# A decoder layer on one core: the stretch from the state space's GLU to the second feed-forward in a held order

## The chip, the core and the metric

The kernel runs on one core of a Trainium2 chip. Its engines each run their own instruction queue: PE (TensorE, matrix products), DVE (VectorE), ACT (ScalarE), POOL (GpSimd) and SP (SyncE, which here only issues DMAs). The metric is the device time of one execution in microseconds, the median of several runs.

## The reference

One layer for one sequence of 1024 tokens and width 1024, all in float32: a feed-forward half-step, a mixing step, and a second feed-forward half-step. Each is normed before and after and modulated by columns computed from a vector `c`.

```python
h = modulate(rms_norm(x, g_pre_ff1[l]), sh1, sc1)
f = swiglu(h, w1_gate[l], w1_up[l], w1_down[l])
x = x + 0.5 * ga1[:, None, :] * rms_norm(f, g_post_ff1[l])

h = modulate(rms_norm(x, g_pre_mix[l]), sh2, sc2)
proj = h @ w_in[l]
...
ssm = s5_ssm(u, ...)          # ends: y = gelu(y); y = y * sigmoid(y @ w_glu + b_glu)
mixed = jnp.concatenate([rms_norm(attn, g_attn_out[l]), rms_norm(ssm, g_ssm_out[l])], axis=-1)
mixed = mixed @ w_out[l]
x = x + ga2[:, None, :] * rms_norm(mixed, g_post_mix[l])

h = modulate(rms_norm(x, g_pre_ff2[l]), sh3, sc3)
f = swiglu(h, w2_gate[l], w2_up[l], w2_down[l])   # (silu(h @ w_gate) * (h @ w_up)) @ w_down
x = x + 0.5 * ga3[:, None, :] * rms_norm(f, g_post_ff2[l])
```

## The kernel before

Every large product is made three times in a reduced form of float32: each operand is split into a high part, an ACT copy (`L69`), and a low part, a DVE subtraction (`L70`), and `mm3` issues high by high, high by low and low by high (`L74` to `L76`). One `mm3` over 512 columns is three matmuls.

On-chip memory is cut into named slots (`a0` to `a27`, `q0` to `q7`, `h0` to `h7`, `r0` to `r3`, `w0` to `w3`, `t0`, `t1`, `c0`), and PE's accumulator memory into banks `b0` to `b7`. A new tile in a slot waits until the old one's last reader is done. Most of the program's order is chosen by a scheduler that replays a timeline. Code inside `pinned(...)` keeps, on every engine, the order in which it is written. SP's queue is in order: a DMA that waits for its slot holds those behind it.

The stretch that is changed has these steps, for eight tiles of 128 tokens:

- *GLU.* Four weight blocks (`late.conv(4)` to `late.conv(7)`) times the split `y_hl`, in two halves of 512 tokens: eight results, each through a sigmoid (`L1214`), a product with `y_t` (`L1215`), a split into `mix_s` and a square summed into `sqs` (`L1221`, `L1222`). The second half of `w_out` comes through `shares`: load, ACT scaling (`L777`), DVE low part (`L778`).
- *Shares.* `share(t)` multiplies tile t of `mix_s` with `w_out`, two halves of four `mm3`; DVE adds it to the attention's share `acc[t]` (`L1254`), ACT squares it (`L1256`), DVE multiplies by the gate row (`L1257`).
- *Joined.* `joined(p)` norms a pair of tiles, adds the residual `X[t]` (`L1266`, slots `a10`, `a11`, `a13` in turn), stores it (`L1267`), squares it (`L1268`), norms again and scales `acc[t]` (`L1272`). `rsqrt` (`L144` to `L148`) is one ACT square root and four small DVE instructions.
- *Turn.* `turn(c, k)` transposes a block of 128 columns of tiles 4c to 4c + 3 on PE (`L1278`), and ACT writes it, modulated, into `hf[k]` (`L1279`).
- *First products.* The second feed-forward's gate and up products take seven Strassen products per pair of output blocks, but the first pair takes eight plain ones. `first(r, c)` is four `first_part`s of four `mm3` each; r is the token half and c the width half. `block(r, c, k)` splits their operands from `hf`. `first(0, ·)` needs only tokens 0 to 511.
- *The rest.* `rest` walks a list of steps (u, m), one product m of output block u each, 12 matmuls. The second pair, u = 2 and 3, comes as (2, "1"), (3, "1"), (2, "2"), (3, "2"), (2, "5") and so on. `wt.conv(i + 3)` converts weights ahead of step i. When a pair is complete `sums` makes four sums at once (`L535`). The operands `s1` to `s4` are sums of quarters of `hf`, made in `s12` and `s34`. A hook turns eight columns of `w_ada` into modulation columns (`L169`), on every second step from step 9.

Before, this stretch from the GLU to `first(1, 0)` is written without `pinned`, and the scheduler interleaves it.

## Time and profile before

| | |
|---|---|
| median of 3 runs | 1674.44 us (1672.31, 1674.44, 1674.67) |
| the profiled execution | 1673.76 us |
| its span | 1671.6 us, 21995 instructions |
| PE busy | 1641.9 us, 98% of the span |
| DVE, ACT, POOL busy | 1225.6, 818.2, 52.5 us |
| mean granted PE clock | 0.996 |
| moved by DMA | 248.53 MB, 149 GB/s on average |

The span runs from the first instruction to the last of the profiled execution; its own time has 2.2 us more. A row of the time order gives start, duration, engine, line, operation, result and operands, and in brackets the idle time before it with what ended it. A group's row gives the number of instructions, their busy time in us, the mean of one in ns, and the idle time before them. Line numbers are those of the kernel before.

### The profile page before, as it was taken

What the parts mean: (1) busy time and instruction counts of PE and PEld (TensorE: products, weight loads), DVE (VectorE), ACT (ScalarE), POOL (GpSimd) and SP (SyncE); (2) the same over time, 40 slices, a digit from 0 to 9 for tenths busy, and PEclk for the clock granted to TensorE, in tenths of its full rate; (3) what the DMA queues carried; (4) which work ended last, traced back from release to release, by engine and by line L of the source; (5) the groups of instructions that cost most, each with busy time, mean ns of one, the idle gap of its engine ahead of it and who ended that gap; (6) DMA issues with size and microseconds to landing.
All of it is one profiled execution on the core that took longest, in us unless ns stands there. A gap on an engine that the chain in (4) does not pass through costs nothing.

```text
span 1671.6 us, 21995 instructions
## 1 busy us (share of the span) xinstructions
PE 1641.9 (98%) x7715; PEld 1347.5 (81%) x7715; DVE 1225.6 (73%) x2277; ACT 818.2 (49%) x1601; POOL 52.5 (3%) x108
## 2 busy tenths in 40 slices
PE   8999999999999999999999998999999999999998
PEld 7878888787788888877887786878888888888886
DVE  6889998789969758758757475877656666578585
ACT  6643333463345458738753558533333333355462
POOL 0001110001100000000000000000000000000000
PEclk9999999999999999999999999999999999999999
DMA  9256762244396334520142225332322333593344
GB/s 368 81 208 230 254 227 99 95 146 152 123 331 243 115 118 145 210 101 26 51 145 65 97 102 199 121 144 95 107 95 95 118 116 114 163 364 104 107 141 136
DMA packets 110913, 248.53 MB, mean 149 GB/s; under 512 B 11962, under 2 KB 27618, under 8 KB 110803
## 3 DMA queue, kind: packets, MB, share of 16 engines
q1 hardware_dynamic: 101074, 213.60, 36.9%
q0 software_dynamic: 9152, 32.49, 5.8%
q8 instruction: 60, 0.98, 0.2%
q10 hardware_dynamic: 576, 1.05, 0.2%
q14 instruction: 51, 0.41, 0.1%
HBM read 187.35 MB, written 59.75 MB: 148 GB/s over the span
## 4 chain that ended last, share of the span: by engine, by line
PE 90%; DVE 5%; ACT 3%; issue 1%; DMA 1%; SPq 0%; DVEq 0%; ACTq 0%
PE b L74 27%; PE b L76 27%; PE b L75 27%; PE b L988 1%; PE b L886 1%; PE b L989 1%; PE b L990 1%; PE b L935 1%; DVE h L535 1%; PE b L1110 1%; DVE w L70 1%; PE b L1114 1%; PE b L1624 1%; ACT q L1533 1%; PE b L1068 0%
## 5 line engine op out<-in xcount | busy, mean ns | idle before, releaser
L74 PE MATMUL b<-a,w 128*128 128x512 f32 x1260 | 493.6, 393 | 6.0 <-ACT w L69 3.3
L76 PE MATMUL b<-a,w 128*128 128x512 f32 x1260 | 492.1, 391 | 1.8 <-DVE w L70 1.5
L75 PE MATMUL b<-a,w 128*128 128x512 f32 x1260 | 491.8, 390 | 1.3 <-DVE a L70 1.0
L74 PEld LDWEIGHTS b<-a,w 128*128 128x128 f32 x1260 | 237.4, 189 | 59.6 <-ACT w L69 4.9
L76 PEld LDWEIGHTS b<-a,w 128*128 128x128 f32 x1260 | 237.0, 188 | 53.9 <-DVE w L70 5.1
L75 PEld LDWEIGHTS b<-a,w 128*128 128x128 f32 x1260 | 237.0, 188 | 50.0 <-DVE a L70 1.5
L70 DVE TENSOR_TENSOR w<-r,w 128x512 fp32r<-128x512 f32 (+1 forms) x208 | 144.5, 696 | 132.1 <-ACT w L69 131.7
L75 PE MATMUL b<-w,r 128*128 128x512 f32 x528 | 205.5, 389 | 0.0
L76 PE MATMUL b<-w,r 128*128 128x512 f32 x528 | 205.4, 389 | 0.0
L74 PE MATMUL b<-w,r 128*128 128x512 f32 x528 | 182.0, 389 | 0.0
L69 ACT CAST w<-r 128x512 fp32r<-128x512 f32 (+1 forms) x208 | 129.0, 622 | 80.3 <-DVE r L403 67.7
L69 ACT CAST r<-a 128x512 fp32r<-128x512 f32 x110 | 68.4, 623 | 146.1 <-PE b L76 104.5
L70 DVE TENSOR_TENSOR r<-a,r 128x512 fp32r<-128x512 f32 x110 | 75.7, 689 | 75.9 <-ACT r L69 75.8
L75 PEld LDWEIGHTS b<-w,r 128*128 128x128 f32 x528 | 99.1, 188 | 20.7 <-DVE w L70 0.2
L74 PEld LDWEIGHTS b<-w,r 128*128 128x128 f32 x528 | 99.1, 188 | 20.6
L76 PEld LDWEIGHTS b<-w,r 128*128 128x128 f32 x528 | 99.1, 188 | 20.5
L69 ACT CAST w<-t 128x512 fp32r<-128x512 f32 (+1 forms) x114 | 69.9, 613 | 80.4 <-DVE t L406 29.9
L70 DVE TENSOR_TENSOR w<-t,w 128x512 fp32r<-128x512 f32 (+1 forms) x114 | 77.9, 683 | 31.1 <-ACT w L69 30.9
L560 ACT ACTIVATE h<-h 128x512 f32<-128x512 f32 x60 | 38.0, 633 | 121.7 <-DVE h L572 121.7
L572 DVE TENSOR_TENSOR h<-h,b 128x512 f32<-128x512 f32 x120 | 82.2, 685 | 20.6 <-PE b L76 18.6
L70 DVE TENSOR_TENSOR w<-a,w 128x512 fp32r<-128x512 f32 x110 | 75.3, 685 | 0.0
L74 PE MATMUL b<-a,a 128*128 128x512 f32 x182 | 72.2, 398 | 0.4 <-ACT h L1214 0.4
(419 smaller groups left out, 2437.5 us busy)
## 6 DMA issues: line engine op xcount, KB each, us to landing
r<-in_w_gu SPq DMA_DIRECT2D x87, 512.0 KB, 4.2
g_d<-h SPq DMA_DIRECT2D x154, 256.0 KB, 2.2
a<-g_d SPq DMA_DIRECT2D x110, 256.0 KB, 2.7
q<-in_w_ada POOLq DMA_DIRECT2D x48, 512.0 KB, 4.6
a<-in_w_d SPq DMA_DIRECT2D x88, 256.0 KB, 5.4
a<-in_w_ada SPq DMA_DIRECT2D x24, 512.0 KB, 9.1
a<-in_x SPq DMA_DIRECT2D x12, 512.0 KB, 5.3
x_d<-a SPq DMA_DIRECT2D x12, 512.0 KB, 3.2
```

What stands on the lines that cost most here:

```text
L69: act.copy(hi, src)
L70: eng.tensor_tensor(lo, src, hi.bitcast(F32), op=SUB)
L74: pe.matmul(psum, wh, xh, start=first, stop=False, skip_group_check=goes_on)
L75: pe.matmul(psum, wh, xl, start=False, stop=False, skip_group_check=goes_on)
L76: pe.matmul(psum, wl, xh, start=False, stop=last, skip_group_check=goes_on)
L535: dve.tensor_tensor(d, x, y, op=op)
L560: act.activation(dst, src, AF.Silu)
L572: dve.tensor_tensor(dst, dst, pb, op=ADD)
L886: pe.matmul(pb[kv][:, m % 2, ks], qT[m][rows, t * P : (t + 1) * P], kT[rows, (t + 1 - nk) * P : (t + 1) * P], start=True, stop=True,)
L935: pe.transpose(pt[:, m, :], pr[4 * kv + m][:, b * P : (b + 1) * P], ident)
L988: pe.matmul(pb, hh, wh, start=k == 0, stop=False)
L989: pe.matmul(pb, hh, wl, start=False, stop=False)
```

## The change

From the GLU on everything is inside `pinned`: `glu` and `both_shares` write out one order for all engines. In it

- all eight `X` tiles have slots of their own, and are loaded ahead;
- `rsqrt` can issue another piece of work between its root and its reciprocal, and `norm` takes the second norm of one pair and the first of another in one go;
- part of the scalings and of the blocks from `turn` moves from ACT to DVE;
- the first token half's transposes stand around share 7, and the second half's behind `first(0, 1)`, between the four first steps of the second pair, which stand ahead of `first(1, 0)`. Their weights have slots `a0` to `a3`;
- both token halves of the first pair use banks `b0` to `b3`;
- `s3` and `s4` are made in the rest's steps 4, 6 and 7, in exchanged slots;
- the pairs' sums are made one per step, those of the first pair from step 16 on;
- the modulation columns come from step 15 on, four in 14 steps, through two slots instead of six;
- `late.conv(4)`, `late.conv(5)` and `shares.load(4)` stand earlier in `middle`, and some slots are others.

```diff
-    def rsqrt(v, n):
+    def rsqrt(v, n, beside=None):
         act.activation(s, v, AF.Sqrt)
+        if beside:
+            beside()
         dve.reciprocal(y, s)
...
+        def rest(self, hook, pin, begin=0):
+            for i, (u, m) in enumerate(self.wt.seq):
+                if i >= begin:
+                    pin(self.wt.conv, i + 3)
+                    pin(self.step, u, m)
+                    if self.todo:
+                        pin(self.todo.pop(0))
+                    hook(i)
...
+            late.conv(4)
+            shares.load(4)
             ss_state(3)
...
-            late.conv(4)
-            shares.load(4)
             out_a(5)
+            late.conv(5)
...
+        def glu():
+            for j in range(8):
...
+                act.activation(y2, pb, AF.Sigmoid, bias=b_glu[:, m : m + 1])
                 dve.tensor_tensor(y2, y2, y_t[m][:, tk], op=MUL)
+                if j:
+                    glu_out(j - 1)
+                if j in (0, 1, 3, 5):
+                    shares.conv((0, 1, 3, 5).index(j))
+                if j in (2, 4):
+                    late.conv(5 + j // 2)
+                if j == 4:
+                    wt.load(0, 0)
+        X_TAGS = "q4", "q5", "q6", "q7", "a10", "a11", "a13", "a27"
...
+        def scaled(p, second=dve):
             for i in range(2):
+                t, r = 2 * p + i, R[p, 1][:, i : i + 1]
+                if i and second is dve:
+                    dve.tensor_scalar(acc[t], X[t], r, None, op0=MUL)
+                else:
+                    act.activation(acc[t], X[t], AF.Identity, scale=r)
+        def turned_in(c, k):
+            if k % 2 and (c == 0 or k < 4):
+                dve.tensor_scalar(dst, src, scale, shift, op0=MUL, op1=ADD)
+            else:
+                act.activation(dst, src, AF.Identity, scale=scale, bias=shift)
...
+        def both_shares():
...
+            share_all(4)
+            joined(3)
+            norm([(1, 0), (0, 1)], lambda: gated(3))
+            scaled(0, act)
+            share_all(5)
...
+            share_all(6)
+            norm([(1, 1)], lambda: gated(4))
+            scaled(1)
+            joined(5)
...
+            turn(0, 0)
+            turn(0, 1)
+            share(7, 0, range(4))
+            norm([(2, 0)], lambda: gated(5))
...
+            share(7, 1, range(4))
+            x_load(7)
...
+            for u, i in ((2, 0), (3, 0), (2, 1), (3, 1)):
+                wt.load(u, i)
+            g2.block(0, 1, 3)
+            added(2)
+            gated(7)
+            added(3)
+            for k in range(4):
+                g2.first_part(0, 1, k, (0, 1))
...
+            norm([(3, 1), (2, 1)], lambda: wt.conv(1))
+            scaled(2)
+            scaled(3)
+            wt.conv(2)
+            g2.step(2, "1")
+            turn(1, 0)
+            turn(1, 1)
...
+            g2.first_done(0)
+            wt.conv(3)
+            g2.step(3, "1")
...
+            g2.step(2, "2")
...
+            g2.step(3, "2")
...
+            g2.first(1, 0)
+            for k in range(4):
+                g2.block(1, 1, k)
+            g2.s1(0, 1, 2, 3)
+            g2.s2(0, 1, 2, 3)
+            wt.conv(8)
+            g2.first(1, 1)
+            g2.first_done(1, False)
...
     def hook3(i):
-        if i < 5:
+        if i == 4:
+            g2.s3(0, 1, 2, 3)
+        if i == 16:
+            z = slot("q2", [2, 512])
+            g2.todo.extend(g2.sums(0, [z[:, 1], g2.st[0, 1, 0], z[:, 0], g2.st[0, 0, 1]], True))
+        if i in (6, 7):
+            g2.s4(2 * i - 12, 2 * i - 11)
+        if i < 15:
             return
...
-        if last_raw and i > 8 and i % 2:
+        if last_raw and i % 14 in (5, 7, 9, 11):
             ada_block(*last_raw.pop(0), last_c[0])
...
-    g2.rest(lambda i: pinned(hook3, i), pinned)
+    g2.rest(lambda i: pinned(hook3, i), pinned, 4)
```

Three places of the resulting order. The first is SP's queue around the residual tiles, `x1_d` in memory; before:

```order
L379 DMA h0_1522_8965<-in_w2_gu 128x512
L379 DMA h1_1523_8966<-in_w2_gu 128x512
L1267 DMA x2_d_92<-a10_1467_8683 128x1024
L1267 DMA x2_d_92<-a11_1474_8720 128x1024
L1248 DMA a10_1492_8819<-x1_d_91 128x1024
L1267 DMA x2_d_92<-a13_1479_8755 128x1024
L1248 DMA a11_1497_8854<-x1_d_91 128x1024
L1267 DMA x2_d_92<-a10_1492_8819 128x1024
L1248 DMA a13_1510_8918<-x1_d_91 128x1024
```

and now (tiles 0 to 3, in `q4` to `q7`, are loaded ahead of these rows):

```order
L1268 DMA a10_1470_8697<-x1_d_91 128x1024
L1268 DMA a11_1471_8699<-x1_d_91 128x1024
L1268 DMA a13_1472_8701<-x1_d_91 128x1024
L1318 DMA x2_d_92<-q4_1453_8627 128x1024
L1318 DMA x2_d_92<-q5_1454_8629 128x1024
L1318 DMA x2_d_92<-q6_1455_8631 128x1024
L1318 DMA x2_d_92<-q7_1456_8633 128x1024
L1268 DMA a27_1539_9045<-x1_d_91 128x1024
L376 DMA r1_1562_9168<-in_w2_gu 128x1024
```

The loads no longer alternate with the stores whose slots they take, and the second pair's first raw weight stands behind tile 7. The second place is ACT's queue around the last pair's scaling (`a6` and `a8` are `acc[6]` and `acc[7]`); before:

```order
L1279 ACTIVATE q5_1458_8635<-b6_1557_9129,modc_77,gsc_78 128x512
L69 CAST a21_1561_9186<-q5_1458_8635 128x512
L1268 ACTIVATE a8_1405_8400,s1528_8998<-a11_1543_9071 128x1024
L144 ACTIVATE s1550_9098<-s1549_9096 128x2
L1279 ACTIVATE q6_1459_8636<-b7_1558_9147,modc_77,gsc_78 128x512
L1272 ACTIVATE a6_1397_8361<-a10_1526_8995,s1551_9099 128x1024
L1272 ACTIVATE a8_1405_8400<-a11_1543_9071,s1551_9099 128x1024
L69 CAST a22_1562_9189<-q6_1459_8636 128x512
L1279 ACTIVATE q7_1460_8637<-b6_1559_9153,modc_77,gsc_78 128x512
```

and now:

```order
L1319 ACTIVATE a6_1400_8367,s1531_9010<-a13_1472_8701 128x1024
L1319 ACTIVATE a8_1405_8400,s1531_9010<-a27_1539_9045 128x1024
L146 ACTIVATE s1568_9242<-s1567_9240 128x4
L71 CAST a0_1570_9245<-r1_1562_9168 128x512
L1327 ACTIVATE a4_1378_8240<-a10_1470_8697,s1569_9243 128x1024
L1327 ACTIVATE a6_1400_8367<-a13_1472_8701,s1569_9243 128x1024
L71 CAST a1_1571_9256<-r2_1563_9170 128x512
L589 COPY h2_1573_9272<-b4_1572_9259 128x512
L1343 ACTIVATE q0_1516_8963<-b6_1574_9274,modc_77,gsc_78 128x512
```

One root serves two pairs, the first token half's blocks (`q5` to `q7`) are gone from between, and the casts of the step weights `a0` and `a1` stand around the scalings. The third place is DVE's queue behind the second pair's last product; before:

```order
L564 TENSOR_TENSOR h0_1655_9795<-h0_1655_9795,b1_1623_9557 128x512
L535 TENSOR_TENSOR h7_1644_9693<-h2_1621_9551,h0_1655_9795 128x512
L535 TENSOR_TENSOR h3_1624_9570<-h0_1655_9795,h4_1633_9630 128x512
L535 TENSOR_TENSOR h5_1636_9649<-h3_1624_9570,h2_1621_9551 128x512
L535 TENSOR_TENSOR h1_1659_9817<-h6_1642_9676,h5_1636_9649 128x512
L169 ISA q0_1640_9658,modc_77<-q0_1640_9658,c0_1637_9651,cols_76 128x1024
L169 ISA modc_77 128x1
L70 TENSOR_TENSOR w0_1660_9827<-t0_1658_9802,w0_1660_9827 128x512
```

and now:

```order
L577 TENSOR_TENSOR q3_1643_9757<-q3_1643_9757,b5_1579_9297 128x512
L545 TENSOR_TENSOR q1_1631_9651<-h2_1573_9272,q3_1643_9757 128x512
L72 TENSOR_TENSOR w0_1647_9780<-t0_1645_9762,w0_1647_9780 128x512
L545 TENSOR_TENSOR h3_1580_9310<-q3_1643_9757,h6_1619_9577 128x512
L72 TENSOR_TENSOR w1_1650_9800<-r2_1638_9702,w1_1650_9800 128x512
```

The weight's low part now stands behind one sum instead of four and a modulation column.

More of the change, by code (lines that the diff above doesn't have):

```diff
@@ L599, in tile_layer @@
+        def rest(self, hook, pin, begin=0):
[6 more added lines that the diff above has]
+                    hook(i)
+            for one in self.todo:
+                pin(one)
     NH_F = NF // 2
@@ new lines, in mix, with glu_out @@
+        hf, Y2 = [], {}
+        g2 = start(hf)
+        wt = g2.wt
+        def glu_out(j):
+            m, tk, y2 = j // 2, halves[j % 2], Y2.pop(j)
+            split(mix_s[m][0][:, tk], mix_s[m][1][:, tk], y2)
+            if m == 0:
+                act.activation(sqs[:, tk], y2, AF.Square)
+            else:
+                s2 = slot(s_rot(), [512])
+                act.activation(s2, y2, AF.Square)
+                dve.tensor_tensor(sqs[:, tk], sqs[:, tk], s2, op=ADD)
+        def glu():
+            for j in range(8):
+                m, tk = j // 2, halves[j % 2]
+                if j % 2 == 0:
+                    gh, gl = late.get(4 + m)
+                pb = bank(("b0", "b1", "b6", "b7")[j % 4])
@@ new lines, in mix, with x_load, share @@
+        X_TAGS = "q4", "q5", "q6", "q7", "a10", "a11", "a13", "a27"
+        def x_load(t):
+            X[t] = slot(X_TAGS[t], [D])
+            sp.dma_start(X[t], x_d[1][t])
+        def share(t, dh, ms):
+            if ms[0] == 0:
+                X["p", t, dh] = bank(f"b{(2 * t + dh + 2) % 6}")
+            tk = slice(t * P, (t + 1) * P)
+            for m in ms:
+                mm3(X["p", t, dh], mix_s[m][0][:, tk], mix_s[m][1][:, tk], wo[m][0][:, halves[dh]], wo[m][1][:, halves[dh]], m == 0, m == 3)
@@ new lines, in share_all, with joined @@
+        def share_all(t):
+            for dh in range(2):
+                share(t, dh, range(4))
+        def joined(t):
+            p = t // 2
+            if t % 2 == 0:
+                if p not in N:
+                    N[p] = small(4, "s4")
+                X["ss", p] = small(4, "s4")
+            for dh in range(2):
+                f = acc[t][:, halves[dh]]
+                dve.scalar_tensor_tensor(f, X.pop(("p", t, dh)), rstd_s[:, t : t + 1], f, op0=MUL, op1=ADD)
+                i = 2 * dh + t % 2
+                act.activation(slot(j_rot(), [512]), f, AF.Square, accum_out=X["ss", p][:, i : i + 1])
@@ new lines, in gated, with norm @@
+        def gated(t):
+            dve.tensor_tensor(acc[t], acc[t], grow[0], op=MUL)
+        def norm(of, beside):
+            p = of[0][0]
+            if of[0][1] == 0:
+                ss = X.pop(("ss", p))
+                dve.tensor_tensor(N[p][:, 0:2], ss[:, 0:2], ss[:, 2:4], op=ADD)
+            c = [(2 if x and q < 3 else 0) for q, x in of]
+            n = N[3 if p == 3 else p + of[0][1]]
+            v = small(2 * len(of), "rsv")
+            dve.tensor_scalar(v, n[:, c[0] : c[-1] + 2], 1.0 / D, EPS, op0=MUL, op1=ADD)
+            r = rsqrt(v, 2 * len(of), beside)
+            for i, k in enumerate(of):
+                R[k] = r[:, 2 * i : 2 * i + 2]
@@ L1274, in turn @@
         def turn(c, k):
[L1276 removed]
+            pt = bank(("b6", "b7")[k % 2], [4, P])
             for i in range(4):
                 pe.transpose(pt[:, i, :], acc[4 * c + i][:, k * P : (k + 1) * P], ident)
[L1279 to L1287 removed]
@@ L1288, in mix @@
-        share(4)
-        joined(1)
-        share(5)
-        for k in range(4):
-            turn(0, k)
-            g2.block(0, 0, k)
-        wt.load(0, 0)
-        wt.load_halves(1, 0, ("h0", "h1"))
-        share(6)
-        joined(2)
-        wt.first(0)
-        share(7)
-        joined(3)
+            X["t", c, k] = pt.rearrange("p t q -> p (t q)")
+        def turned_in(c, k):
+            dst, src = g2.q(c, k // 4, k % 4), X.pop(("t", c, k))
+            scale, shift = gsc[:, 2, k : k + 1], mod(6)[:, k : k + 1]
+            if k % 2 and (c == 0 or k < 4):
+                dve.tensor_scalar(dst, src, scale, shift, op0=MUL, op1=ADD)
+            else:
+                act.activation(dst, src, AF.Identity, scale=scale, bias=shift)
@@ L1301, in mix @@
+        pinned(glu)
+        wo = [shares.get(i) for i in range(4)]
         if stage == "mix":
             return None
-        g2.first(0, 0, lambda k: [turn(0, 4 + 2 * k + i) for i in range(2)] if k < 2 else None)
-        for k in range(4):
-            g2.block(0, 1, k)
-        wt.first(1)
-        g2.first(0, 1, lambda k: [turn(1, 2 * k + i) for i in range(2)])
-        for k in range(4):
-            g2.block(1, 0, k)
-        g2.first(1, 0)
-        for k in range(4):
-            g2.block(1, 1, k)
+        pinned(both_shares)
@@ L1713, in tile_layer @@
     sp.dma_start(sink, a["sinks"].partition_broadcast(P))
-    def second_half(g):
-        for i in range(2):
-            g.wt.load(2, i)
-        for i in range(2):
-            g.wt.load(3, i)
-        g.first_done(0)
-        g.wt.conv(3)
-        g.s12()
-        g.first(1, 1)
-        g.first_done(1)
-        g.s34()
     def second_half_1():
```

313 lines of the change are left out of this document (177 added, 136 removed).

## The prediction

> **What bounds the kernel now.** I read the page's busy table first, then the busy time by stretches around the stage that the change touches, the idle rows of TensorE (PE) in time order, the chain that ended last, and last the groups by line for prices.
>
> ```profile
> PE 1641.9 (98%) x7715; PEld 1347.5 (81%) x7715; DVE 1225.6 (73%) x2277; ACT 818.2 (49%) x1601; POOL 52.5 (3%) x108
> ```
>
> PE is the bound of the whole kernel: it stands still for 1671.6 − 1641.9 = 29.7 us. A change of order can win only from that. The edited stage, from the GLU to the second pair's products, runs from 945 to 1118 us:
>
> ```profile
> 945.00:957.00 12.00, 10.98 (x47) 8.23 (x46) 8.04 (x10) 11.69 (x17) 0.00 (x0) 1.00 0.62 240
> 957.00:1010.00 53.00, 53.00 (x244) 44.02 (x244) 41.93 (x84) 30.84 (x68) 0.00 (x0) 1.00 0.33 119
> 1010.00:1020.00 10.00, 6.20 (x25) 4.44 (x24) 5.38 (x10) 8.55 (x17) 0.00 (x0) 0.83 0.59 210
> 1020.00:1038.00 18.00, 15.13 (x72) 12.04 (x71) 9.11 (x23) 15.45 (x25) 0.56 (x1) 0.91 0.55 205
> 1038.00:1115.00 77.00, 77.00 (x351) 63.79 (x350) 58.35 (x94) 38.03 (x66) 4.24 (x8) 1.00 0.38 133
> 1115.00:1118.00 3.00, 1.93 (x9) 1.29 (x8) 3.00 (x6) 1.22 (x3) 0.00 (x0) 1.00 0.57 212
> ```
>
> The columns are the stretch, its length, PE, weight loads, DVE (VectorE), ACT (ScalarE), POOL, the granted clock, the DMA share and GB/s. PE idles 12.00 − 10.98 = 1.02 us in the GLU, 3.80 + 2.87 us between the shares and the first products, and 1.07 us at 1115; together 8.76 us. In the middle the clock also fell: 6.20 us at 0.83 and 15.13 us at 0.91 lose 1.05 + 1.36 = 2.41 us. The stops themselves are eleven rows, of which these are five, first and last among them:
>
> ```profile
> 954.88 0.50 PE L74 MATMUL b<-q,h 128*128 128x512 f32 x1 [0.58 <-ACT h L69]
> ...
> 1014.28 0.47 PE L1278 MATMUL b<-ident,r 128*128 128x128 f32 x1 [1.88 <-ACT q L1279]
> ...
> 1018.68 0.50 PE L75 MATMUL b<-a,w 128*128 128x512 f32 x1 [1.03 <-DVE a L70]
> ...
> 1034.77 1.97 PE L1278 MATMUL b<-ident,a 128*128 128x128 f32 x8 [0.86 <-ACT q L1279]
> ...
> 1117.32 0.50 PE L76 MATMUL b<-a,w 128*128 128x512 f32 x1 [1.07 <-DVE w L70]
> ```
>
> Busy rows overlap, so each stop is longer than its row says. Unhindered, these two starts lie 24 matmuls apart:
>
> ```profile
> 999.10 0.39 PE L74 MATMUL b<-a,a 128*128 128x512 f32 x1
> 1004.54 0.39 PE L74 MATMUL b<-a,a 128*128 128x512 f32 x1
> ```
>
> 5.44 / 24 = 0.227 us from start to start, with rows of 0.39, so every stop hides another 0.16 us: 11 × 0.16 = 1.8. What the stage loses is 8.76 + 2.41 + 1.8 = **13.0 us**, and that is the most that this change can win by the listed rows. The 24 matmuls are one token tile's share; a product or a `first_part` is 12, 2.72 us.
>
> Why PE waits there, from the chain that ended last:
>
> ```profile
> 1009.83 1.05 ACT r L1272
> 1010.90 4.51 DMA a<-x_d
> 1015.53 1.30 DVE a L1266
> 1016.87 0.94 issue
> ...
> 1031.35 2.19 ACT a L1272 x2
> ```
>
> The residual tiles `X` rotate through three slots, so the load for token tile 6 starts only when tile 3 has been scaled (1009.83), takes 4.51 us, and everything in the last pair's two norms comes after it. Its scaling (1031.35) ends 23 us after the last share product at 1010.5. Over that time PE has only `first(0, 0)`, 48 matmuls or 10.9 us, and a few transposes. The stop at 1117 is another thing:
>
> ```profile
> 1111.99 0.68 DVE L564 TENSOR_TENSOR h<-h,b 128x512 f32<-128x512 f32 x1
> 1112.71 2.75 DVE L535 TENSOR_TENSOR h<-h,h 128x512 f32<-128x512 f32 x4
> 1115.37 1.28 DVE L169 CUSTOM_DVE_ANT_0 q<-q,c,cols 128x1024 f32<-128x1024 f32 x1
> ...
> 1116.58 0.69 DVE L70 TENSOR_TENSOR w<-t,w 128x512 fp32r<-128x512 f32 x1
> ```
>
> The pair's four sums and a modulation column stand in DVE's queue ahead of the weight's low part for which PE waits.
>
> **The change, part by part.** PE's instructions are the same in number and shape, so nothing is added there; only stops count. Prices:
>
> ```profile
> L1254 DVE SCALAR_TENSOR_TENSOR a<-b,rstd_s,a 128x512 f32<-128x512 f32 x8 | 5.9, 745 | 1.3 <-PE b L76 1.3
> L70 DVE TENSOR_TENSOR a<-q,a 128x512 fp32r<-128x512 f32 x8 | 5.4, 688 | 3.9 <-ACT a L69 3.9
> L1266 DVE SCALAR_TENSOR_TENSOR a<-a,s,a 128x1024 f32<-128x1024 f32 x4 | 5.1, 1284 | 8.4 <-ACT a L69 4.4 <-DMA a<-x_d 4.0
> L1257 DVE TENSOR_TENSOR a<-a,a 128x1024 f32<-128x1024 f32 x4 | 4.9, 1222 | 1.4 <-ACT h L1256 1.4
> L145 DVE RECIPROCAL s<-s 128x2 f32<-128x2 f32 (+1 forms) x9 | 1.2, 162 | 1.2 <-ACT s L144 1.2
> L925 DVE TENSOR_SCALAR a<-a,s 128x256 f32<-128x256 f32 x40 | 11.5, 350 | 0.2
> L1279 ACT ACTIVATE q<-b,modc,gsc 128x512 f32<-128x512 f32 x10 | 7.4, 768 | 0.0
> L69 ACT CAST a<-q 128x512 fp32r<-128x512 f32 x9 | 5.4, 610 | 0.0
> L1272 ACT ACTIVATE a<-a,s 128x1024 f32<-128x1024 f32 x4 | 4.4, 1142 | 0.5 <-DVE s L148 0.5
> L1268 ACT ACTIVATE a<-a 128x1024 f32<-128x1024 f32 x4 | 4.2, 1051 | 3.3 <-DVE a L1266 3.3
> L1256 ACT ACTIVATION_READ_ACCUMULATOR h<-a 128x1 f32 x8 | 1.5, 187 | 0.0
> L1214 ACT ACTIVATE h<-b,cols 128x512 f32<-128x512 f32 x2 | 1.4, 688 | 0.2 <-PE b L76 0.2
> L1221 ACT ACTIVATE h<-h 128x512 f32<-128x512 f32 x4 | 2.5, 634 | 1.1 <-DVE a L1222 1.1
> ```
>
> *Eight slots for X.* Tiles 0 to 6 are loaded before the first norm, tile 7 once share 7 has released its slot. The 4.51 us load leaves the chain. Tile 7's load has some six `first_part`s (16 us) until `added(3)` wants it.
>
> *First group's transposes before share 7.* `turn(0, 0)` stands behind share 6, 6 × 5.44 = 32.6 us after share 0. Until then DVE needs, for tiles 0 to 5 as far as the scaling, 12 × 0.745 + 5 × 1.222 + 4 × 1.284 + 4 × 0.688 + 1.3 + about 18 small ones of 0.16 = 27 us. It fits, with 5 us over, and the stop of 1.88 us at 1014 goes.
>
> *Second group behind `first(0, 1)` and a step.* This is the main term. Between share 7 and `turn(1, 0)` PE now has eight `first_part`s, `step(2, "1")` and four transposed blocks (between 0.23 us, 512 columns at the pace above, and 0.98, half of the row at 1034.77; I take 0.4, nearer the full clock): 9 × 2.72 + 1.6 = 26.1 us. DVE in that time, in its held order: 2 leftovers of low parts and a transposed block (2.1), `joined(7)` 2 × 0.745, two transposed blocks 1.5, nine low parts 6.2, eleven small 1.8, four `added` 5.1, `gated` 1.2, two scalings 2.6: 22.0 us. ACT needs two squares of 512 columns at 0.63 + 0.19 (L1221, and the reading of the sum), 2 × 0.77, 9 × 0.61, four squares at 1.05 + 0.19, 2 × 1.14 and 0.4 of small ones: 16.4. Room is 26.1 − 22.0 = 4.1 us, of which I give half to hand-offs between the two. The scalings on DVE, `tensor_scalar` 128x1024, do not occur before: by L925 they take at most 4 × 0.35 = 1.4 us, by half of that at least 0.7; I take L1266's 1.28. Cover gone, each microsecond of lateness is one of PE.
>
> *Moved to DVE:* six blocks read from PSUM at L1254's 0.745 instead of ACT's 0.768, counted above. *Norms of two pairs at once:* two chains of some six small instructions fewer; off PE's path, nothing.
>
> *The GLU in held order.* Eight products are 96 × 0.227 = 21.8 us. ACT needs 8 × 0.688 + 8 × 0.61 + 8 × 0.634 + 4 × 1.15 (weights, estimated by L1272) + 2 × 0.61 = 21.3 us: almost as much, in a fixed order. The fourth GLU weight is converted behind product 4's sigmoid; I reckon its low part about 0.5 us late (0 to 1.1). That replaces the 1.02 us. `late.conv` and `shares.load` moved up in `middle` wait on SP for the same slots (`w0` to `w3`, free after `out_a(7)`), with nothing urgent behind them: nothing.
>
> *Four products ahead.* Their weights `a0` to `a3` are read from `r1`, `r2`, `r3`, `r0`, of which three hold token tiles until the last transpose of the first group. On SP they stand behind tile 7's load. From there to the first cast PE has 5 `first_part`s less the cast's lead, 10 us; a load takes
>
> ```profile
> r<-in_w_gu SPq DMA_DIRECT2D x87, 512.0 KB, 4.2
> a<-in_w_ada SPq DMA_DIRECT2D x24, 512.0 KB, 9.1
> ```
>
> 4.2 us typically, 9.1 in the worst group. Hidden, though that cast stands on ACT ahead of the second group's scalings. `step(2, "2")` wants its low part just when I reckon it ready: up to 0.6 us.
>
> *Sums and columns later.* The sums come one at a time behind a product, 0.69 beside 2.72 us, and the columns start at step 15. In steps 4 to 13 DVE has 34 instructions, some 23 us beside 27 of PE. The 1117 stop goes (1.07 + 0.16).
>
> Sum: 13.0 won, less 0.5 (GLU) and three narrow places (column sums behind the GLU, `step(2, "2")`, the first block of a group) at half a microsecond each, the size of the 0.58 row: 13.0 − 2.0 = **11.0 us**. The profiled execution took 1673.76 us (span 1671.6 and 2.2 around it), which gives 1662.8; it stood 0.7 below the median of 1674.44, so I say **1663.4 us**.
>
> **Rivals.** *A: the held order hands its gain half back.* A held queue lets nothing past a waiting instruction. In the second group's chain some ten results go from ACT to DVE or back, and where the rows above show such waits they are 1.03 us (1018) and 0.86 (1034). Ten at their mean, 0.95, are 9.5, against a room of 4.1: 5.4 us of new stop, 1668.8. For it: ACT in the GLU at 98%. Against: most of the ten meet an operand finished long ago.
> The Trainium skill's page "TensorE: Matmul & The Clock Gate", in the section on the array's architecture, says that ACT and DVE are strict first-in-first-out queues, which speaks against any order held by hand; this trace agrees, DVE's L70 at 1116.58 coming only after L169. By its Part 1 the clock halves after an idle window of about 3.4 us; by it the 2.41 us would not be there to win, and the time would be 1665.8. Before had stops of 1.88 at most and still fell to 0.83, so the row decides.
>
> *B: the loss only changes place.* DVE gets the blocks, the scalings and the sums; if its 22 and 23 us become 27 to 32 because scalings and PSUM reads are half as slow again, PE stops about 5 us in each place, and the result is 1673. Against: DVE is at 41.93 of 53 us in the shares and 9.11 of 18 after.
>
> *C: slower, by the raw weights.* The cast of `a0` holds ACT, with it both scalings, `turn(1, 0)` and PE. If `r1` landed later than 10 us after its issue, PE would stand one for one; from 10 + 11 + 3.4 = 24 us the kernel is slower by more than 0.2%. If the four loads ran one after the other at the 9.1 us of the worst group and `r1` came last, 36 us: 26 us of stop, 1689. Against: the 4.2.
>
> **How the numbers follow.** 0.2%, 3.3 us, is about what tells a change from none here. My forecast (stops of 0 to 4 us in all) gets 0.75, A 0.12, B 0.06, C 0.07. A lies on the faster side but for 0.01. Faster is 0.75 + 0.11 = 0.86, the same 0.06 + 0.01 = 0.07, slower 0.07. The range begins at 1659.8, where no new stop is left (1661.4) and another 1.6 us of stops too short for the rows go too, and ends with A, 1669.0: it leaves out part of A, all of B and C.
>
> **What would show it.** Right: between 945 and 1115 PE's stretches are full at clock 1.00; no wait for `x_d`; `turn(1, 0)` follows `step(2, "1")` at once; no stop at the end of the first pair's products. Wrong: PE waiting for ACT's scalings or a transposed block (A), DVE full with PE idle (B), ACT's cast waiting for a DMA of `in_w2_gu` (C), or a new idle stretch behind step 4, where s3 and s4 are made.

## The result, and the profile after

The changed kernel takes 1660.0 us (median of four runs, 1659.7 to 1661.83), the kernel before beside it 1674.53 (1672.31 to 1674.67): a ratio of 0.9919, with a 95% interval of 0.9904 to 0.9935. That is 14.5 us won where 11.0 were forecast, inside the forecast range, 3.4 us below the forecast time of 1663.4 and 0.2 us above the range's lower end.

The busy row of the page after, and the same stretches as in the prediction (stretch, length, PE, weight loads, DVE, ACT, POOL, granted clock, DMA share, GB/s):

```profile
PE 1639.1 (99%) x7715; PEld 1347.3 (81%) x7715; DVE 1231.3 (74%) x2276; ACT 811.7 (49%) x1590; POOL 52.4 (3%) x108
```

```profile
945.00:957.00 12.00, 11.90 (x53) 9.54 (x52) 8.77 (x12) 9.58 (x15) 0.00 (x0) 1.00 0.56 215
957.00:1010.00 53.00, 52.72 (x248) 43.74 (x248) 41.42 (x77) 32.23 (x67) 0.00 (x0) 1.00 0.39 149
1010.00:1020.00 10.00, 10.00 (x49) 8.34 (x48) 7.90 (x12) 6.32 (x14) 0.00 (x0) 1.00 0.16 54
1020.00:1038.00 18.00, 18.00 (x85) 14.99 (x84) 13.47 (x26) 11.81 (x20) 0.56 (x1) 1.00 0.68 263
1038.00:1115.00 77.00, 76.80 (x355) 63.62 (x354) 60.61 (x96) 41.10 (x70) 1.07 (x2) 1.00 0.23 83
1115.00:1118.00 3.00, 3.00 (x15) 2.47 (x14) 2.36 (x5) 0.92 (x3) 0.00 (x0) 1.00 0.90 348
```

PE has as many instructions as before and stands still for 20.9 us of the span instead of 29.7. Of the stage's 173 us it is idle for 0.58 instead of 8.76, and the clock is 1.00 throughout, where it had been 0.83 and 0.91 in the middle. PE's rows in time order hold two stops in the whole stage (a third wait, 0.10 us in the first stretch, is too short to be marked), and the second group's transposes follow the step without one (the eight rows of `turn(1, 0)` and `turn(1, 1)` read as one):

```profile
960.25 0.50 PE L78 MATMUL b<-q,h 128*128 128x512 f32 x1 [0.28 <-DVE h L72]
1038.60 0.39 PE L78 MATMUL b<-a,a 128*128 128x512 f32 x1
1038.83 1.03 PE L1333 MATMUL b<-ident,a 128*128 128x128 f32 x8
1044.18 0.50 PE L78 MATMUL b<-a,a 128*128 128x512 f32 x1 [0.20 <-DVE a L72]
```

What they wait for is ready just in time. The rows are the last scalings of the second group, on DVE and on ACT, and between them the cast of the weight of `step(2, "1")`, the first of the four products ahead:

```profile
1035.19 1.41 DVE L1325 TENSOR_SCALAR a<-a,s 128x1024 f32<-128x1024 f32 x2
1033.15 0.60 ACT L71 CAST a<-r 128x512 fp32r<-128x512 f32 x1
1035.25 2.19 ACT L1327 ACTIVATE a<-a,s 128x1024 f32<-128x1024 f32 x2 [1.50 <-DVE s L152]
```

ACT ends at 1035.25 + 2.19 = 1037.44, PE arrives at 1038.83: 1.4 us to spare.

The profiled execution was the slowest of the four (1661.83). It lost time ahead of the change: the same transposes of an earlier stage start 1.61 us later than in the profile before.

```profile
859.24 1.97 PE L1057 MATMUL b<-ident,w 128*128 128x128 f32 x16 [0.36 <-ACT w L994]
```

```profile
860.85 1.97 PE L1077 MATMUL b<-ident,w 128*128 128x128 f32 x16 [0.36 <-ACT w L1014]
```

So from profile to profile the span shrinks by 1671.6 − 1660.0 = 11.6 us, and what lies behind that point by 13.2 (from 812.4 to 799.2).

### The profile page after: what moved, and what is told of

Same layout as the page of the kernel before. It is cut to its first block, busy times and chain, and to the rows that moved or that the text cites. A ratio compares the mean times of both kernels' runs of the same rounds, so it can differ in the third digit from the quotient of the medians.

```text
span 1660.0 us, 21960 instructions
## 1 busy us (share of the span) xinstructions
PE 1639.1 (99%) x7715; PEld 1347.3 (81%) x7715; DVE 1231.3 (74%) x2276; ACT 811.7 (49%) x1590; POOL 52.4 (3%) x108
## 4 chain that ended last, share of the span: by engine, by line
PE 93%; DVE 3%; ACT 2%; issue 0%; DMA 0%; SPq 0%; DVEq 0%; ACTq 0%
PE b L76 28%; PE b L78 28%; PE b L77 28%; PE b L1008 1%; PE b L906 1%; PE b L1794 1%; PE b L1009 1%; PE b L1010 1%; PE b L955 1%; PE b L1130 1%; PE b L1134 1%; ACT q L1703 1%; DVE h L545 1%; PE b L1088 0%; DMA a<-in_w_ada 0%
## 5 line engine op out<-in xcount | busy, mean ns | idle before, releaser
L76 PE MATMUL b<-a,w 128*128 128x512 f32 x1244 | 488.3, 393 | 6.0 <-ACT w L71 3.3
L78 PE MATMUL b<-a,w 128*128 128x512 f32 x1244 | 486.4, 391 | 0.8 <-DVE w L72 0.5
L77 PE MATMUL b<-a,w 128*128 128x512 f32 x1244 | 485.3, 390 | 0.2 <-DVE a L1771 0.2
L76 PEld LDWEIGHTS b<-a,w 128*128 128x128 f32 x1244 | 234.2, 188 | 58.5 <-ACT w L71 4.7
L78 PEld LDWEIGHTS b<-a,w 128*128 128x128 f32 x1244 | 234.2, 188 | 52.4 <-DVE w L72 3.6
L77 PEld LDWEIGHTS b<-a,w 128*128 128x128 f32 x1244 | 234.3, 188 | 48.1 <-DVE a L1771 0.5
L585 DVE TENSOR_TENSOR h<-h,b 128x512 f32<-128x512 f32 x103 | 70.5, 684 | 16.8 <-PE b L78 15.2
L573 ACT ACTIVATE h<-h 128x512 f32<-128x512 f32 x51 | 32.3, 633 | 101.4 <-DVE h L585 101.4
L76 PE MATMUL b<-a,a 128*128 128x512 f32 x198 | 78.4, 396 | 0.0
L78 PE MATMUL b<-a,a 128*128 128x512 f32 x198 | 77.3, 390 | 0.2 <-DVE a L72 0.2
```

Source lines behind the costliest of these rows:

```text
L76: pe.matmul(psum, wh, xh, start=first, stop=False, skip_group_check=goes_on)
L77: pe.matmul(psum, wh, xl, start=False, stop=False, skip_group_check=goes_on)
L78: pe.matmul(psum, wl, xh, start=False, stop=last, skip_group_check=goes_on)
L573: act.activation(dst, src, AF.Silu)
L585: dve.tensor_tensor(dst, dst, pb, op=ADD)
```

## The experiments

Theory T at the outset: the gain is the work that PE has in front of each group of transposes (its cover), and X loads that no longer wait. Each kernel was timed beside the kernel before, whose median was 1673.2 to 1674.5 in these sets, so the ratios are compared. The fourth column is the difference of a ratio from 0.9919 times 1674 us. Each ratio is uncertain by up to about 2.5 us and such a difference by about 3.5; differences in the text are these unless another is named. The last column compares one profiled execution of each, from the transposes of the earlier stage to the end, with the 799.2 us of the changed kernel; what an execution loses ahead of them is not in it.

| kernel | median us | ratio to before, 95% interval | us against the changed kernel | the same in the profiles |
|---|---|---|---|---|
| kernel before | 1674.53 | 1 | +13.6 | +13.2 |
| changed kernel | 1660.00 | 0.9919 (0.9904 to 0.9935) |  |  |
| `cover_behind` | 1674.96 | 1.0008 (0.9998 to 1.0017) | +14.9 | +14.3 |
| `step_behind` | 1662.32 | 0.9934 (0.9920 to 0.9949) | +2.5 | +1.5 |
| `slots_alone` | 1670.13 | 0.9983 (0.9974 to 0.9993) | +10.7 | +9.8 |
| `slots_head` | 1671.33 | 0.9989 (0.9979 to 0.9998) | +11.7 | +10.9 |
| `four_slots` | 1661.16 | 0.9930 (0.9913 to 0.9948) | +1.8 | +0.8 |
| `scheduler` | 1671.38 | 0.9987 (0.9978 to 0.9997) | +11.4 | +12.8 |
| `held_head` | 1665.01 | 0.9951 (0.9936 to 0.9965) | +5.4 | +4.0 |
| `before_held` | 1704.99 | 1.0194 (1.0177 to 1.0211) | +46.0 | +45.1 |
| `act_scales` | 1661.55 | 0.9934 (0.9918 to 0.9950) | +2.5 | +1.5 |
| `norms_single` | 1665.28 | 0.9952 (0.9936 to 0.9968) | +5.5 | +4.6 |
| `pair_sums` | 1666.29 | 0.9959 (0.9944 to 0.9973) | +6.7 | +6.0 |
| `weights_ahead` | 1658.82 | 0.9915 (0.9900 to 0.9930) | -0.7 | -1.2 |

### The cover in front of the second group

`cover_behind`:

```diff
-            for k in range(4):
-                g2.first_part(0, 1, k, (0, 1))
...
-            g2.step(2, "1")
             turn(1, 0)
             turn(1, 1)
             turned_in(1, 0)
             turned_in(1, 1)
+            for k in range(4):
+                g2.first_part(0, 1, k, (0, 1))
+            g2.step(2, "1")
```

> The changed kernel with first(0, 1) and step(2, "1") issued behind turn(1, 0) and turn(1, 1) instead of ahead; all else as changed. Theory T (the gain is the work that PE now has in front of the second group's transposes): in the changed kernel turn(1, 0) follows step(2, "1") at 1038.83 and the last scaling ended at 1037.44, so there are 1.4 us to spare; PE loses 60 matmuls of cover, 60 x 0.227 = 13.6 us, and stands 13.6 - 1.4 = 12.2 us in front of turn(1, 0). With 0 to 2.5 us for a lower clock behind the stop: 1672 to 1675, back at the time before. Rival S (the eight slots for X are the gain, the order of PE's products is not): the scalings are early whatever PE does, a stop of at most 3 us, 1660 to 1663.

`step_behind` moves `g2.step(2, "1")` alone to that place.

> The changed kernel with step(2, "1") alone issued behind turn(1, 0) and turn(1, 1). Theory T: 12 matmuls, 2.72 us, less of cover against 1.4 us to spare: PE stands 1.3 us (1.0 to 1.6) in front of turn(1, 0); the time is 1661 to 1662, less than three rounds tell apart, so the trace decides. If the spare time is larger than the 1.4 us read from the starts: no stop.

PE's rows at `turn(1, 0)`, of `cover_behind` and then of `step_behind`:

```profile
1034.24 0.69 PE L1333 MATMUL b<-ident,a 128*128 128x128 f32 x2 [11.06 <-ACT a L1327]
1035.28 1.54 PE L1333 MATMUL b<-ident,a 128*128 128x128 f32 x6 [0.35 <-ACT a L1327]
```

```profile
1034.86 0.44 PE L1333 MATMUL b<-ident,a 128*128 128x128 f32 x2 [0.20 <-ACT a L1327]
1035.90 0.87 PE L1333 MATMUL b<-ident,a 128*128 128x128 f32 x6 [0.60 <-ACT a L1327]
```

With the cover behind, PE stands for 11.06 + 0.35 us at that place (12.2 expected), the granted clock is 0.51 from there to 1039.5, and the whole gain is gone: 14.9 us. With the step alone behind, the two waits come to 0.80 us where 1.3 were expected from the spare 1.4 us, and the time rises by 2.5 (1.5 in the profiles) with intervals that overlap. Theory T holds for the cover.

### The slots for X

`slots_alone`, an edit of the kernel before:

```diff
-        hf = [slot(f"q{k}", [D]) for k in range(NK)]
+        hf = []
...
-            X[t] = slot(("a10", "a11", "a13")[t % 3], [D])
+            X[t] = slot(("q4", "q5", "q6", "q7", "a10", "a11", "a13", "a27")[t], [D])
...
         share(5)
+        hf.extend(slot(f"q{k}", [D]) for k in range(NK))
```

> The kernel before with eight slots for X instead of three (tile 7 in a slot that share 7 frees), nothing else changed, order by the scheduler. Before, DVE waits 4.01 us at 1015.53 and 4.40 us at 1027.61 for loads of X; the second group's scalings ended at 1033.5, about 10.5 us after PE had run out of first(0, 0). Theory T: 8.4 us of these waits go, some 2 us of lateness and part of the first group's stops stay, as do the GLU's 1.0 and the 1.2 at 1117: 8 to 10 us won with the clock, 1664.5 to 1666.5. Rival O (the order alone is what wins; the loads are only the last of many waits in the chain): the waits turn into waits for ACT and DVE, at most 3 us won, 1671 to 1674. Rival S: 12 us or more won, below 1662.5.

PE's stops from 1009 to 1040:

```profile
1012.05 0.44 PE L1278 MATMUL b<-ident,r 128*128 128x128 f32 x2 [0.60 <-ACT r L1272]
1014.79 0.33 PE L1278 MATMUL b<-ident,r 128*128 128x128 f32 x1 [2.30 <-ACT q L1279]
1016.67 2.07 PE L74 MATMUL b<-a,w 128*128 128x512 f32 x4 [0.56 <-ACT a L69]
...
1033.14 0.50 PE L74 MATMUL b<-a,a 128*128 128x512 f32 x1 [0.97 <-ACT a L69]
```

The four waits at the second group's transposes are gone, as expected, and one for a block of it, 0.97 us, has come. The first group's stay, and the gain over the kernel before is 2.8 us (0.17%), not 8 to 10: I had counted DVE's waits for loads (8.4 us) as if PE had stood for all of them, while PE's stops at the second group were 2.87 us in the kernel before. What holds the first group up stands in ACT's queue, in front of the block (`L1279`) for which PE waits 2.30 us:

```profile
1011.90 1.04 ACT L1268 ACTIVATE a<-a 128x1024 f32<-128x1024 f32 x1
...
1012.94 1.04 ACT L1268 ACTIVATE a<-a 128x1024 f32<-128x1024 f32 x1
...
1013.98 0.76 ACT L1279 ACTIVATE q<-b,modc,gsc 128x512 f32<-128x512 f32 x1
```

Two squares of the next pair, for transposes that come at 1031, stand ahead of a block wanted at once.

The reverse, `four_slots`, keeps the changed order and takes the slots away:

```diff
-        X_TAGS = "q4", "q5", "q6", "q7", "a10", "a11", "a13", "a27"
+        X_TAGS = "a10", "a11", "a13", "a10", "a11", "a13", "a10", "a27"
...
             scaled(0, act)
+            x_load(3)
+            x_load(4)
...
             scaled(1)
+            x_load(5)
+            x_load(6)
```

(the earlier loads of tiles 3 to 6 are dropped).

> The changed kernel with X in the three slots of before, but for tile 7, which keeps its own: tiles 3 and 4 are loaded once tiles 0 and 1 are scaled, 5 and 6 once 2 and 3 are. Eight slots without the order won 3.2 us; this asks what the order wins nearly without the slots. Theory T (order and cover carry most): tile 0 is scaled at 995.2 in the changed kernel, its load takes 4.5 to 6.5 us, so the second of added(1), due at 996.5, waits 3.5 to 5.2 us; the scalings of pair 1 end at about 1007 instead of 1002.8, 1 to 2.7 us behind PE's arrival at turn(0, 0); the second group comes some 1 us late; with the clock 2 to 5 us lost, 1662 to 1665. Rival S (without the slots the order is worth little): waits pile up behind each load in the held queues, 1668 or more.

```profile
996.41 1.28 DVE L1317 SCALAR_TENSOR_TENSOR a<-r,s,a 128x1024 f32<-128x1024 f32 x1 [2.41 <-DMA a<-x_d]
```

DVE waits 2.41 us for tile 3, less than I expected, and no stop of PE follows: the 1.8 us by which the time is longer can't be told from nothing, and the stretches of PE are as full as in the changed kernel. In this order the slots are worth little.

### Held order, written order

`scheduler` calls `glu()` and `both_shares()` instead of `pinned(glu)` and `pinned(both_shares)`.

> The changed kernel, written in the same order, but its GLU and shares not held: the scheduler may move instructions past each other, as in the kernel before. Theory T (slots and cover make the gain, holding the order does not): within 3 us of the changed kernel, 1659 to 1664. Rival H (the held order makes the gain): the stops come back at the second group and the time is over 1668.

Theory T in its first form falls here: with slots, cover and written order all there, but not held, 11.4 us of the gain are gone. PE's longest stop:

```profile
1018.17 1.11 PE L1333 MATMUL b<-ident,r 128*128 128x128 f32 x4 [6.70 <-ACT r L1327]
```

It goes back to the start of the chain of norms; in `held_head` below, which holds this start, PE waits for no scaling. The first joined tile (`L1290`, `L1254` in the kernel before: DVE adds a share to the attention's) needs the norm of the column sums (`L158`), and that needs the sums from PE. PE's last column sums and DVE from there on, without the held order:

```profile
978.34 0.95 PE L1355 MATMUL b<-ones,a 128*128 128x1 f32 x8
```

```profile
978.83 0.69 DVE L72 TENSOR_TENSOR w<-h,w 128x512 fp32r<-128x512 f32 x1 [4.49 <-ACT w L71]
979.44 0.16 DVE L158 TENSOR_SCALAR s<-b 128x8 f32<-128x8 f32 x1
...
982.12 0.69 DVE L72 TENSOR_TENSOR w<-h,w 128x512 fp32r<-128x512 f32 x1 [0.76 <-ACT w L71]
982.73 1.40 DVE L1290 SCALAR_TENSOR_TENSOR r<-b,rstd_s,r 128x512 f32<-128x512 f32 x2
```

and in the changed kernel:

```profile
969.45 1.84 PE L1355 MATMUL b<-ones,a 128*128 128x1 f32 x16
```

```profile
972.81 1.41 DVE L1290 SCALAR_TENSOR_TENSOR r<-b,rstd_s,r 128x512 f32<-128x512 f32 x2
```

The first joined tile is 9.9 us later, 8.0 of it in the column sums, which end at 979.29 instead of 971.29. The scheduler had put share products between the GLU's last products, and more of them ahead of the sums and among them. The other 1.9 us come behind the sums, where the scheduler had put the first weights' casts and low parts. The low part at 978.83, for a cast that had waited 4.57 us for its load, keeps the norm back by no more than 0.15 us; the one at 982.12 stands between the norm and the joined tile. In the kernel before the sums were late too, ending at 978.03, and with them the first joined tile:

```profile
979.55 1.41 DVE L1254 SCALAR_TENSOR_TENSOR r<-b,rstd_s,r 128x512 f32<-128x512 f32 x2
```

Against that the changed kernel's 972.81 is 6.7 us earlier, 8.3 with the 1.6 that its profile lost ahead of the stage: a head start for the whole chain of norms.

`held_head` holds the order only up to the first pair's norm:

```diff
             norm([(0, 0)], lambda: wt.first_op(1, 1, 0))
+
+        def rest_of_shares():
             share_all(3)
...
         pinned(both_shares)
+        rest_of_shares()
```

> The changed kernel with its order held as far as the first pair's norm, norm([(0, 0)]), and everything from share_all(3) on left to the scheduler. In the kernel with nothing held (1671.4 us) the column sums stand behind two shares and the first joined tile starts at 982.73 instead of 972.81; a weight's cast that waits 4.57 us for its load stands ahead of that norm; turn(0, 0) then waits 6.70 us for a scaling, and the second group does not wait at all. Theory H1 (order matters at this one place, the head of the stage): 1659.5 to 1663, turn(0, 0) without a stop. Rival H2 (the order must be held throughout): over 1665, with stops at the second group or among the first products.

```profile
1011.92 0.33 PE L1333 MATMUL b<-ident,r 128*128 128x128 f32 x1 [0.74 <-DVE q L1341]
1012.99 0.33 PE L1333 MATMUL b<-ident,r 128*128 128x128 f32 x1 [0.41 <-ACT q L1343]
1014.63 1.64 PE L76 MATMUL b<-a,w 128*128 128x512 f32 x4 [0.98 <-ACT a L71]
```

It lies between: holding the GLU and the head brings 6.0 us of the order's 11.4 (8.8 of 12.8 in the profiles), and 5.4 (4.0) are lost among the first group's blocks, where casts of later weights and squares again stand ahead of the blocks that PE waits for. Neither H1 nor H2 alone.

`slots_head` was to bring the head into the kernel with `slots_alone`'s edit:

```diff
-            share(t)
+            pinned(share, t) if t < 2 else share(t)
...
-        wt.first(0)
+        pinned(wt.first, 0)
```

> The kernel before with eight slots for X and, besides, shares 0 and 1 and the first weights' split held in their written order, so that the column sums and their norm go ahead of the weights' casts; everything else by the scheduler. Eight slots alone gave 1670.1: the second group's stops went, while turn(0, 0) to turn(0, 3) still lose 3.46 us and the clock 1.5. Theory H1 + slots (late column sums make the first group's stops, late X loads the second group's): the first joined tile starts some 5 us earlier than 982.3, the first group's stops go, 1664.5 to 1667. Rival (the first group waits for something else): 1669 to 1671.

It did not do what it was made for: the column sums stay behind other shares and end at 979.32, against 978.13 in `slots_alone`, whose profile had lost 1.2 us less ahead of the stage. Only the weights' low parts are gone from between the sums and the first joined tile, which starts at 980.84, 1.4 us earlier than in `slots_alone`. PE is idle for 1.3 us more before 1005, and its stops at the first group are the same 0.60, 2.30 and 0.56 us. What earlier column sums alone would be worth in that kernel stays open.

`before_held` wraps the kernel before's GLU and its shares in `pinned`, as they are written there.

> The kernel before, with its GLU and its shares up to the second group's blocks held in the order in which they are written there, nothing else changed. Theory T (the order that is written is what wins, holding it is only what lets it be written): in the old writing order each pair's whole chain (norm, added, squares, norm, scalings, some 12.5 us) stands right behind its share, and turn(0, 0) follows 5.4 us of PE work later: a stop of about 7 us there, about 9 in front of first(0, 0), whose weights' casts stand behind joined(2), and about 6 in front of turn(1, 0) with the loads of X; together some 22 us against 14 lost before, with the clock 1680 to 1690. Rival H (holding alone wins, because the scheduler misjudges): 1668 or less.

```profile
1015.33 0.48 PE L1281 MATMUL b<-ident,r 128*128 128x128 f32 x1 [8.28 <-ACT r L1275]
...
1039.86 0.79 PE L74 MATMUL b<-a,w 128*128 128x512 f32 x1 [6.42 <-ACT w L69]
...
1054.96 0.47 PE L1281 MATMUL b<-ident,r 128*128 128x128 f32 x1 [5.77 <-ACT q L1282]
```

32.5 us (1.94%) slower than before, 15 beyond what I expected: holding is no gain by itself. The old text, held, stops where expected (`turn(0, 0)`, the first products, the blocks) and in the GLU besides. A held queue pays for every wrong place: the load of the weight for which PE waits 6.42 us landed at 1020.29, but its cast comes at 1039.21 on ACT, behind two scalings that had waited for their norm. The Trainium skill's page "TensorE: Matmul & The Clock Gate", in the section on the array's architecture, says that ACT and DVE are strict first-in-first-out queues; this cast agrees.

### Smaller parts

`act_scales`:

```diff
-        def scaled(p, second=dve):
+        def scaled(p, second=act):
...
-            if k % 2 and (c == 0 or k < 4):
+            if False:
```

> The changed kernel with all scalings and all transposed blocks on ACT, as before, in the same order. Theory T: two scalings of 1.1 us more stand in ACT's queue in front of turn(1, 0): its last one ends at about 1039.6 instead of 1037.4, against 1038.83, so a stop of 0.8 us there; blocks come up to 0.8 us later, up to 0.5 us at the first block of each group: 1660.5 to 1662. Rival: ACT is at 18 of 30 us there and takes it without a stop, 1660.

2.5 us (1.5 in the profiles), with an interval that overlaps the changed kernel's. The eight transposes take 1.36 us instead of 1.03, since the fourth scaling ends among them, and a new wait comes behind, for the high part of `step(2, "2")`'s weight:

```profile
1042.83 0.50 PE L76 MATMUL b<-a,a 128*128 128x512 f32 x1 [0.56 <-ACT a L71]
```

The size is about the expected one; half of it lies at a place that I had not named.

`norms_single`:

```diff
-            norm([(1, 0), (0, 1)], lambda: gated(3))
+            norm([(0, 1)], lambda: gated(3))
             scaled(0, act)
+            norm([(1, 0)], None)
...
             added(2)
-            gated(7)
+            norm([(2, 1)], lambda: gated(7))
+            scaled(2)
             added(3)
...
-            norm([(3, 1), (2, 1)], lambda: wt.conv(1))
-            scaled(2)
+            norm([(3, 1)], lambda: wt.conv(1))
             scaled(3)
```

> The changed kernel with each pair's norms made one by one, in the order added(2), norm, scaled(2), added(3), norm, scaled(3), instead of both second norms at once. Theory T: added(3) stands behind the first norm's hand-offs, some 1.8 us later, but only one scaling is left behind the last norm, 1.1 us less: the scalings end about 0.7 us later than 1037.44, inside the 1.4 us to spare; no stop, 1660 to 1661. Rival (the joined norms are what keeps the chain short): a stop of 2 us or more at turn(1, 0).

5.5 us lost (4.6 in the profiles) where none were expected. PE's rows at the stop and behind it, and the last scaling:

```profile
1035.46 0.39 PE L78 MATMUL b<-a,a 128*128 128x512 f32 x1
1037.91 0.50 PE L76 MATMUL b<-a,a 128*128 128x512 f32 x1 [2.06 <-ACT a L71]
...
1040.08 0.63 PE L78 MATMUL b<-a,a 128*128 128x512 f32 x1
1040.51 0.63 PE L76 MATMUL b<-a,a 128*128 128x512 f32 x1
...
1042.13 0.39 PE L77 MATMUL b<-a,a 128*128 128x512 f32 x1
```

```profile
1039.34 1.15 ACT L1327 ACTIVATE a<-a,s 128x1024 f32<-128x1024 f32 x1 [1.48 <-DVE s L152]
```

The last scaling ends at 1040.49, 3.05 us later than in the changed kernel, though PE is no later. The weight of `step(2, "1")`, cast beside the last norm at 1037.26 instead of 1033.15, is late too, and PE stops for it before it comes to the transposes. How much of the stop a cast at another place would have saved, this run doesn't show. From 1035.46 the next start lies 2.45 us away instead of 0.227; then ten starts take 4.22 us instead of 2.27, because the clock has fallen. 2.22 + 1.95 = 4.2 of the 4.6 us that the profile lost stand in these rows.

`pair_sums`:

```diff
-            self.bank_of, self.later, self.U, self.todo = bank_of, n == 2, {}, []
+            self.bank_of, self.later, self.U, self.todo = bank_of, False, {}, []
...
-        if i < 15:
+        if i < 5:
             return
...
-        if last_raw and i % 14 in (5, 7, 9, 11):
+        if last_raw and i > 8 and i % 2:
```

> The changed kernel with the later pairs' four sums made at once at the product that ends a pair, and the modulation columns from step 9 on every odd step, as before; the first pair's sums stay late. Theory T: the stop of 1.07 us in front of a product between 1100 and 1125 comes back, 1.2 us, 1661 to 1662; three rounds hardly tell that, so the trace decides. Rival: DVE has room there in the changed order and nothing stops, 1660.

6.7 us lost (6.0 in the profiles) instead of 1.2. (With the first pair's four sums made at once as well, right behind `first(1, 1)`, the order is a deadlock: `sums_at_once` has no time, and here those sums stay late.) DVE's queue, with the last of the four sums first, and PE's stop:

```profile
1105.42 0.69 DVE L545 TENSOR_TENSOR q<-q,h 128x512 f32<-128x512 f32 x1
1106.03 1.28 DVE L173 CUSTOM_DVE_ANT_0 q<-q,c,cols 128x1024 f32<-128x1024 f32 x1
...
1107.24 0.69 DVE L72 TENSOR_TENSOR w<-t,w 128x512 fp32r<-128x512 f32 x1
```

```profile
1107.98 0.79 PE L78 MATMUL b<-a,w 128*128 128x512 f32 x1 [2.21 <-DVE w L72]
```

The mechanism is that of the prediction: four sums and a column ahead of a weight's low part. But the stop is twice the old one. Another one of 0.49 us comes at 1093.8, behind a modulation column, and behind the long one PE is slow: the granted clock is 0.53 from 1107.98 to 1111.60, which costs some 1.7 us.

`weights_ahead`, the changed kernel with three casts moved up:

```diff
+                if j in (2, 4):
+                    late.conv(5 + j // 2)
                 if j:
                     glu_out(j - 1)
...
-                if j in (2, 4):
-                    late.conv(5 + j // 2)
...
+            wt.conv(3)
             g2.first_done(0)
-            wt.conv(3)
```

> The changed kernel with late.conv(6) and late.conv(7) placed ahead of the GLU's glu_out of their turn, and wt.conv(3) ahead of first_done(0): the three products that still wait in the changed kernel (0.25, 0.45 and 0.36 us beyond their pace, each for a weight's low part) get their weights earlier. Theory T: 0.5 to 1.1 us won, 1659.0 to 1659.6, and no stop over 0.1 us left between 945 and 1115. Rival (ACT and DVE are so full in the GLU that what goes ahead puts something else behind): the 0.45 turns into a wait for y_hl or a bank, 1660 to 1661.

```profile
945.00:957.00 12.00, 12.00 (x55) 9.93 (x54) 10.37 (x15) 10.31 (x17) 0.00 (x0) 1.00 0.38 138
957.00:1010.00 53.00, 53.00 (x252) 44.28 (x251) 41.60 (x78) 31.87 (x67) 0.00 (x0) 1.00 0.41 149
...
1038.00:1115.00 77.00, 77.00 (x352) 63.79 (x352) 61.65 (x99) 40.28 (x70) 1.06 (x2) 1.00 0.27 96
```

PE is full in every stretch of the stage, at a clock of 1.00: the last stops are gone. The gain of 0.7 us (1.2 between the medians and in the profiles) is the expected one, though the ratios overlap; the trace shows it, the times alone don't.

## Why the prediction was right, point by point

**The bound and the sum.** PE's stops and the lower clock behind them were the whole matter. The prediction put the loss at 13.0, called that the most that could be won, and put the remainder at 2.0. Measured behind the earlier stage's point the stage won 13.2, and what remains is about 1.1 (0.25, 0.45 and 0.36 us beyond the pace, which `weights_ahead` takes away). So the loss before was about 14.3, 1.3 more than the sum had. By the distances of the starts, an estimate, about 0.6 of that is the lower clock (some 3.0 us instead of 2.41). The rest is hidden in the stops, for which the flat 0.16 us was too little: the start behind a stop is late as well (1019.02 after 1018.68, 0.34 us instead of 0.227). The range's lower end had 1.6 us for stops too short for the rows. Without that allowance the result would lie outside, and with it it is inside by 0.2 us, which is partly luck. 13.2 − 11.0 = 2.2 of the 3.4 us by which the forecast was too high are here; 0.7 is the step from the profile to the median, which did not carry over, and 0.3 the time around the span (2.16 before, 1.83 after).

**The second group, the main term.** Right in kind and size. PE's work from share 7 to `turn(1, 0)` took 26.30 us (26.1 worked out) and it arrives with 1.4 us to spare where I left about 2, and `cover_behind` shows what the cover is worth: everything. The inner terms fit less well. DVE was busy for 19.5 us up to its last scaling instead of 22.0, and it was idle for 4.5 us in that time, mostly waiting for ACT, where half of 4.1 had been set aside; what ends last is a scaling on ACT.

**The first group.** The stop went, but by a step that the working lacked. It counted 27 us of DVE work from share 0 on and did not ask when DVE can begin. The column sums, in the list of narrow places at half a microsecond, are in fact a place where the held order wins: they end 6.7 us earlier, and DVE begins as much earlier. The 5 us over came out as 2.5: the last scaling of pair 1 ends at 1002.8, on ACT, and PE's first transposes start at 1005.3.

**Eight slots.** The load left the chain, and in this order that was worth nothing that could be measured (`four_slots`); alone it is worth 2.8 us (`slots_alone`). The prediction read the chain that ended last rightly, but a link of a chain is not its price.

**Norms of two pairs at once: "off PE's path, nothing".** Nothing was lost by it, but the joined norms are part of the 1.4 us: one by one, with the cast beside the last of them, they cost 5.5. The room of 4.1 us had been worked out with them, and the sentence should have said so.

**Scalings on DVE.** Priced at 1.28, measured at 0.76 (below); on ACT they and the blocks would cost some 2.5 (1.5 in the profiles).

**The GLU.** 0.5 us forecast for the fourth weight, 0.45 measured, and 0.25 at the third, which I had not named.

**Four products ahead.** Hidden. The cast at 1033.15 comes 10.8 us after the load's issue at 1022.39 and waits for no load. Rival C is out.

**Sums and columns later.** The 1.2 us were read from the order before. In the changed order the same backlog would cost 6.7 (6.0 in the profiles). That does not show in the forecast, because the change takes the backlog away in either case.

**Rival A, and the rule against a held order.** No stop of that kind is in the trace. Holding was not the price but the condition: without it 11.4 us are lost. The prices of the parts (14.9, 11.4, 6.7, 5.5) add up to far more than the gain, so none of them is a share of it: each says what is lost when that part alone is missing. Rival B is out too: DVE has 61 of 77 us in the last long stretch and stops nothing.

## What to carry to other kernels

Ask of each engine's chain when it can begin, not only how long it is: a few one-column products that stood behind share products in PE's queue delayed the whole chain of norms by 6.7 us in the kernel before and by 8.0 in `scheduler`. A written and held order is worth as much as its weakest place, so price each part by undoing it in the new order, not by the stop it had in the old one. And when PE is the bound, count a stop of two microseconds twice: the lower clock behind it took 1.95 us after a stop of 2.06 and some 1.7 after one of 2.21.
